# Low-part keys of the second block's attention with 128 rows instead of 64

## The chip, the cores and the metric

The kernel runs on one core of a Trainium2 chip. The metric is the device time of one execution in microseconds (us). Five engines work side by side: TensorE (PE; PEld is its weight load), VectorE (DVE), ScalarE (ACT), GpSimd (POOL) and SyncE (SP), which issues the DMAs.

## What is computed

One forward pass of two transformer blocks over 256 tokens of width 1024. The first block has one layer (a linear recurrence beside sparse attention, then a gated feed-forward). The second has two layers, run over the tokens `x` and a context `ctx` of 256 tokens each. The change lies in the two attentions of the second block's layers: a neighbourhood attention with 4 heads (`A`) and a grouped-query attention with 8 query and 2 key heads (`C`), all of 64 features. The x queries see the keys of x and of the context; the context's queries (first layer only) see the context's alone.

```python
# neighbourhood attention, per row of the grid
s_lat = jnp.einsum('bjqhd,bjykhd->bhjqyk', q_r, k_blk) * scale
s_lat = jnp.where(valid, s_lat + bias, NEG_INF)
s_ctx = jnp.einsum('bjqhd,bchd->bhjqc', q_r, k_ctx) * scale
p = jax.nn.softmax(jnp.concatenate([s_lat, s_ctx], axis=-1), axis=-1)
...
# grouped queries
s = jnp.einsum('bqkgd,bskd->bkgqs', q, k) * (q.shape[-1] ** -0.5)
p = jax.nn.softmax(s, axis=-1)
return jnp.einsum('bkgqs,bskd->bqkgd', p, v)
```

## The kernel before

**Split numbers.** Matmuls take a reduced float32 form (`fp32r`). To keep float32 accuracy, an operand is held as a high part and a low part, the rest that the high part misses, and a product is made of three: high x high, low x high, high x low. In the large projections (`gemm`, L364 to L366) these are three matmuls per tile of 128 rows. A head of the attention has only 64 features, so the queries (`QA`, `QC`) are tiles of 128 rows: rows 0 to 63 hold the high part, rows 64 to 127 the low part. The high-part keys (`KH` for attention A, `CH` for C) lie twice in their 128 rows. So one matmul of 128 rows (L1357) gives high x high plus low x high. The third product, high query x low key, takes the low-part keys (`KL`, `CL`), which fill rows 0 to 63 of a tile allocated with 128 rows (`kv_alloc`): L1362 multiplies rows 0 to 63 of the query tile with rows 0 to 63 of the keys. In the trace the key tiles are named KHa and KLa (attention A) and KHc and KLc (attention C), with a last letter x or c for the tokens that they belong to.

**Units.** `attend` runs over units (head, half of the queries). `soft` makes the scores of 128 queries: for each set of keys 256 columns, by L1357, for attention A's x keys two matmuls for the bias (L1360, L1361), and L1362. So a unit has 2 score matmuls in the context's attention, 4 in x's attention C, 6 in x's attention A. Then VectorE takes the maximum (L1364), ScalarE the exponential and its sum (L1367), VectorE divides (L1368, L1369). `turn`, two units later, transposes the result on TensorE (L1378) and copies it (ScalarE, L1381); after four units, 16 matmuls of the values follow (L1388).

**Where they run.** The context's attention of layer 0 runs from about 804 to 896 us, beside block 1's feed-forward; x's of layer 0 from about 1100 to 1196, beside the context's output projection; x's of layer 1 from about 2075 to 2157. There the only other work is the first half of x's own output projection and what is left of the keys and pooled columns.

**What sets the order.** The program is handed to a scheduler that fixes one order for each engine from a model of its own. The engines then run their lists strictly in order, and wait for each other through semaphores. Scores lie in one set of PSUM buffers (`m`, 4 of them), transposes in another (`f`, 3).

Of the kernel before, what the change touches and what calls it, by code (L numbers as in the profile page):

```python
# [17 lines left out]
PSUM = bass.MemoryType.PSUM  # L18
# [11 lines left out]
# the work of the three mixers: projections, and then what goes beside the units of either attention (a group for each).  # L30
# q, k, v, c, u: projections; V, C, U: what one of their tiles still needs; b: bias; t: a step from outside; s: statistics
# [106 lines left out]
def stat(w, c0, c1):  # L138
    """[K, M] columns c0:c1 as stationary pieces of 128 columns: [M/128, 128, K/128, 128]."""
    w = np.asarray(w)[:, c0:c1]  # L140
    k, m = w.shape
    return np.ascontiguousarray(w.reshape(k // 128, 128, m // 128, 128).transpose(2, 1, 0, 3))


def movp(w):
    """[1024, 512] as moving pieces of 2 row tiles: [4, 128, 2, 512]."""
    w = np.asarray(w)
    return np.ascontiguousarray(w.reshape(4, 2, 128, w.shape[1]).transpose(0, 2, 1, 3))


def upw(a, b):
    """gate and up columns, interleaved by tile: [22, 2, 128, 8, 128]."""
    return np.ascontiguousarray(np.stack([stat(a, 0, FF), stat(b, 0, FF)], 1))


def per_piece(g):
    """column tiles in a down piece of g row tiles"""
    return 1 if g > 4 else 2 if g > 2 else 4


def dnw(w, groups):
    """[2816, 1024]: for each group of row tiles and few column tiles, [128, g, n * 128], one after another."""
    w = np.asarray(w).reshape(NF, 128, 8, 128)
    out, f0 = [], 0
    for g in groups:
        nd = per_piece(g)
        out.append(np.ascontiguousarray(w[f0:f0 + g].reshape(g, 128, 8 // nd, nd * 128).transpose(2, 1, 0, 3)).ravel())
        f0 += g
    return np.concatenate(out)


def adaw(w):
    """[1024, 9216]: pieces [72, 128, 1024] in the order of their use: two modulations at a time, in four parts"""
    w = np.asarray(w).reshape(8, 128, 9216)
    out = []
    for i in range(4):
        a = w[:, :, i * 2048:(i + 1) * 2048]
        for k in range(8):
            out.append(a[k, :, 0:1024])
            out.append(a[k, :, 1024:])  # L180
    for k in range(8):
        out.append(w[k, :, 8192:])
    return np.ascontiguousarray(np.stack(out))
# [82 lines left out]
def build(tc, A, O, dbg=(), stop=None):  # L266
# [32 lines left out]
    f32 = lambda a: a.bitcast(F32)  # L299
# [33 lines left out]
    class Stream:  # L333
# [8 lines left out]
        def load(self, src, a, b, i=0):  # L342
            """a piece as it is; other rings than the usual one take the i-th of many at once"""
            if i < self.nr:
                r = tl(self.raw, [128, 1024], tag="r")
            else:
                r = f32(tl((self.h, self.l)[i % 2], [128, 1024], F32R, tag="hl"[i % 2]))
            rv = r[:, 0:a * b].rearrange("p (a b) -> p a b", a=a)
            self.q.dma_start(rv, src)
            return rv  # L350
# [9 lines left out]
    def gemm(pt, w, m0, m1, xs):  # L360
        """pt += columns m0:m1 of a split stationary piece, over the tiles xs of (hi, lo)"""
        n = len(xs)
        for k in range(n):
            te.matmul(pt, w[0][:, k, m0:m1], xs[k][0], start=k == 0, stop=False)  # L364
            te.matmul(pt, w[0][:, k, m0:m1], xs[k][1], start=False, stop=False)  # L365
            te.matmul(pt, w[1][:, k, m0:m1], xs[k][0], start=False, stop=k == n - 1)  # L366
# [13 lines left out]
    def squares(pp, ps, src, n, late=0, nb=3, scale=None):  # L380
        """sums [128, n / 128] of the squares of src(k), k = 0..7, token-major; the last, late of them, are summed
        by the tensor engine alone"""
        nt = n // 128
        ss = ps(nt)

        def total(sq, first, last):
            for t in range(nt):
                te.matmul(ss[:, t:t + 1], sq[:, t * 128:(t + 1) * 128], ones[:, 0:1], start=first and t == 0, stop=last,
                          skip_group_check=True)

        early = KD - late
        for k in range(KD):
            sq = tl(pp, [128, n], tag="sq", bufs=nb) if k or not early else tl(pp, [128, n], tag="sa", bufs=1)
            s.activation(sq, src(k), AF.Square, scale=scale(k) if scale else 1.0)
            if k == 0:
                acc = sq
            elif k < early:
                g.tensor_tensor(acc, acc, sq, op=OP.add)  # L398
            if k >= early:
                total(sq, k == 0, k == KD - 1)  # L400
            elif k == early - 1:
                total(acc, True, not late)
        return ss

    def stats(pp, ps, src, n, rs, late=0, nb=3):
        """rs [128, n / 128] = 1 / rms of src(k), k = 0..7, token-major"""
# [4 lines left out]
    def rms(pp, ps, src, n, out, late=0, rs=None):  # L411
        """out(k, bc): bc [128, n] is 1 / rms of src(k), k = 0..7, along the columns"""
# [7 lines left out]
        bc = ps(n)  # L420
# [4 lines left out]
    def norm_split(pp, ps, src, n, yh, yl, sc, sh=None, late=0, rs=None):  # L425
        """src * rstd * sc(k) + sh(k) in parts yh, yl"""
# [57 lines left out]
    # ================= block 1 =================  # L484
    def block1(ps, early, ready):
# [8 lines left out]
        # rope tables from the positions  # L494
# [48 lines left out]
        for _ in range(E0):  # L543
            next(early, None)
        with ExitStack() as e:
# [10 lines left out]
            def rope_in(dst, nh, cos, sin, rows=128, pp=pp):  # L556
                """dst [rows, nh, 64] in place"""
# [9 lines left out]
            # token-major queries, then keys and values  # L567
# [57 lines left out]
            # feature-major: receptance, keys, values, low-rank inputs  # L625
# [30 lines left out]
            # compressed keys and values  # L656
# [143 lines left out]
        with ExitStack() as e:  # L800
# [16 lines left out]
            # decay: log w = -e^-0.5 sigmoid(w0 + tanh(w_lat) w2); running sums in each chunk  # L817
# [21 lines left out]
            def head_rstd(sq, scale, eps, floor, neg):  # L839
                """sum of sq over the 64 features of a head -> (.)^-0.5, over the features of the head, in PSUM"""  # L840
# [22 lines left out]
            # negated, normalised keys  # L863
# [15 lines left out]
            # the bonus r . k_mod r_k, over v  # L879
# [9 lines left out]
            # A~ = -kk P_{t-1}, R~ = r P: [pair, token tile, which, token]  # L889
# [20 lines left out]
            # token-major A~, B^, K^, V  # L910
# [20 lines left out]
            # Gram blocks, transposed [j, i]  # L931
# [28 lines left out]
            # (I - L)^-1 by substitution: a partition is (parity of the columns, head, chunk)  # L960
# [92 lines left out]
            # group norm over a head, bonus, gate  # L1053
# [31 lines left out]
    def block1_out(ps, st, before_last):  # L1085
        mix = b1mix
        xr = lambda k: res[:, k, 0:T]
# [1 line left out]
        with ExitStack() as e:  # L1089
# [20 lines left out]
            # the scale of the output norm, and of the norm that follows it on its result  # L1110
# [11 lines left out]
    # ================= block 2 =================  # L1122
# [14 lines left out]
    class Ada:  # L1137
        """modulations of a layer, feature-major: M [128, 9, 8, (x, ctx)], and GS = g (1 + scale) of its three norms"""
# [45 lines left out]
    # each table's rope rows, with the norm's gains (and the queries' 1/8) folded in  # L1184
# [22 lines left out]
    def qkn(pp, src, nh, seg, t, tab, hl):  # L1207
        """heads [128, nh, 64]: norm, rope, split into hl [128, nh, 2, 64]"""
# [28 lines left out]
    def kv_alloc(kp, n):  # L1237
# [4 lines left out]
        o.CL = tl(kp, [128, 2, T], F32R, name="KLc" + n)  # L1242
        o.VA = tl(kp, [128, 2, 256], name="VA" + n)
# [45 lines left out]
    def in_v(l, st, pp, ps, yh, yl, segs, kvs, tab):  # L1289
        """values and keys; returns what is left to do for the keys, a token tile at a time"""  # L1290
# [27 lines left out]
    def in_qc(l, st, pp, ps, yh, yl, seg, t0, tab, QC):  # L1318
        """queries; returns what is left to do, a token tile at a time"""
# [24 lines left out]
    def attend(pp, ps, pst, pso, Q, nh, keys, vals, kvof, mh, ml, bias=None, tick=None):  # L1344
        """keys: [(KH, KL)], vals(i, kt, kv) -> [128, 64]; mh, ml [128, nh / 2, 256]"""
# [5 lines left out]
        def soft(h, t):  # L1351
# [3 lines left out]
            for i, (kh, kl) in enumerate(keys):  # L1355
# [6 lines left out]
                te.matmul(o, q[0:64], kl[0:64, kv], start=False, stop=True)  # L1362
# [39 lines left out]
    class Bias:  # L1402
        """the neighbourhoods' bias and mask of (head, token tile) units, in parts, made some units ahead"""
# [22 lines left out]
    def in_u(l, st, pp, ps, yh, yl, c0, mh, ml):  # L1426
        """pooled columns; returns what is left to do, half of the groups at a time"""
# [34 lines left out]
    def mixer(l, seg, st, qp, side, ps, pin, pst, pso, yh, yl, c0, segs, kvs, tab, mixt, orders, out=True, tick=None, extra=None):  # L1462
        """projections of the sequences segs, attention, pooling and output projection of seg; its columns start at c0"""
# [63 lines left out]
    def norm_mod(l, j, seg, pp, ps, yh, yl, late=0, rs=None):  # L1527
        """modulated norm j of a sequence's residual"""
# [12 lines left out]
    def out_proj(l, seg, st, ps, mixt, half):  # L1541
        """one half of the mixed rows, two column tiles a step"""
# [22 lines left out]
    class Both:  # L1565
        i = 0
# [14 lines left out]
    # the context of block 2's first layer does not wait for block 1: its pools lie at the other end of the memory  # L1581
# [53 lines left out]
    # x, first layer  # L1635
# [37 lines left out]
    # both, to the second layer's projections; x goes ahead of the context at each norm  # L1673
# [79 lines left out]
```

## Time and profile before

| | us |
|---|---|
| median of 3 runs | 2380.18 |
| the runs | 2373.62, 2380.18, 2383.07 |
| span of the profiled execution | 2382.3 |
| TensorE busy | 2283.6 (96%) |
| VectorE busy | 1374.2 (58%) |
| ScalarE busy | 946.8 (40%) |
| GpSimd busy | 361.0 (15%) |

For the profiled execution the page gives the span alone, from the first to the last instruction; its time as a run is not listed. A matmul's busy time is from its start to a modelled end, and one starts before the other has ended, so what it occupies is read from start to start. TensorE has two clock levels, 1.2 and 2.4 GHz; the profile tells the granted share (1.00 or 0.50 of full speed, and a mean where a stretch has both).

### The profile page before, as it was taken

To read this page: it belongs to the slowest core of one execution; us is meant where nothing else is said; L and a number is where in the kernel's file an instruction comes from. 1 tells how busy PE (TensorE), PEld (TensorE's weight loads), DVE (VectorE), ACT (ScalarE), POOL (GpSimd) and SP (SyncE) were. 2 spreads that over 40 slices of the span, in tenths; PEclk is the share of its full clock that TensorE was granted. 3 is DMA by queue.
4 is the path that set the end of the run, shared out by engine and by line. 5 is a ranking of instruction groups with operands and counts; after the bars stand their busy time and mean duration, and the time that the engine had idled before them with its cause. 6 is when DMAs were issued, how large, how long until landed. Compare 5 with 4: busy or idle time off the path is not lost.

```text
span 2382.3 us, 38350 instructions
## 1 busy us (share of the span) xinstructions
PE 2283.6 (96%) x15317; PEld 1964.1 (82%) x15317; DVE 1374.2 (58%) x2442; ACT 946.8 (40%) x1602; POOL 361.0 (15%) x278
## 2 busy tenths in 40 slices
PE   7999987999999899998999999999999999999998
PEld 3687766888999689997778777798888889778998
DVE  4555566358656766677565333357534347855665
ACT  4334422236444454454543222245322235554443
POOL 2125444444101200002010000011000003200000
PEclk9999998999999899997999999999999999989999
DMA  8865544356554145553166434465523245303554
GB/s 295 283 213 177 177 129 145 108 176 225 181 179 166 62 141 176 174 175 104 41 221 223 159 131 165 138 236 187 195 92 98 92 134 178 116 21 100 185 186 131
DMA packets 114929, 376.25 MB, mean 158 GB/s; under 512 B 18464, under 2 KB 24480, under 8 KB 114752
## 3 DMA queue, kind: packets, MB, share of 16 engines
q1 hardware_dynamic: 114752, 373.82, 47.3%
q8 instruction: 120, 1.97, 0.3%
q14 instruction: 57, 0.47, 0.1%
HBM read 372.20 MB, written 1.57 MB: 157 GB/s over the span
## 4 chain that ended last, share of the span: by engine, by line
PE 65%; issue 23%; DVE 6%; DMA 4%; POOL 1%; ACT 1%; SPq 0%; POOLq 0%; DVEq 0%; ACTq 0%
PE m L364 10%; PE m L366 10%; PE m L365 10%; PE f L364 5%; PE f L366 5%; PE f L365 5%; PE f L1163 3%; DMA r<-in_ada 2%; PE o L1388 2%; PE m L1362 2%; PE f L1378 1%; PE m L1357 1%; POOL sa L398 1%; DVE l L357 1%; ACT h L356 1%
## 5 line engine op out<-in xcount | busy, mean ns | idle before, releaser
L356 ACT CAST h<-r 128x1024 fp32r<-128x1024 f32 (+1 forms) x547 | 567.1, 1042 | 1065.4 <-PE m L365 434.9
L357 DVE TENSOR_TENSOR l<-r,h 128x1024 fp32r<-128x1024 f32 (+1 forms) x467 | 572.3, 1229 | 352.2 <-ACT h L356 343.0
L364 PE MATMUL m<-yh,h 128*128 128x256 f32 (+1 forms) x1624 | 490.2, 303 | 2.3 <-ACT h L356 1.1
L366 PE MATMUL m<-yh,l 128*128 128x256 f32 (+1 forms) x1624 | 489.8, 302 | 1.0 <-DVE l L357 1.0
L365 PE MATMUL m<-yl,h 128*128 128x256 f32 (+1 forms) x1624 | 489.5, 302 | 0.0
L364 PEld LDWEIGHTS m<-yh,h 128*128 128x128 f32 x1624 | 310.1, 192 | 25.9 <-ACT h L356 8.1
L366 PEld LDWEIGHTS m<-yh,l 128*128 128x128 f32 x1624 | 310.2, 191 | 19.8 <-issue 7.1
L365 PEld LDWEIGHTS m<-yl,h 128*128 128x128 f32 x1624 | 310.4, 191 | 15.6 <-issue 3.7
L357 POOL TENSOR_TENSOR l<-r,h 128x1024 fp32r<-128x1024 f32 x80 | 194.2, 2432 | 337.7 <-ACT h L356 318.6
L398 POOL TENSOR_TENSOR sa<-sa,sq 128x256 f32<-128x256 f32 x81 | 86.1, 1064 | 1038.5 <-issue 743.6
L365 PE MATMUL m<-hl,h 128*128 128x256 f32 (+1 forms) x738 | 220.1, 302 | 0.0
L366 PE MATMUL m<-hh,l 128*128 128x256 f32 (+1 forms) x738 | 219.9, 303 | 0.0
L364 PE MATMUL m<-hh,h 128*128 128x256 f32 (+1 forms) x738 | 215.6, 304 | 0.1
L364 PE MATMUL f<-yh,h 128*128 128x256 f32 (+1 forms) x624 | 199.6, 320 | 1.8 <-ACT yh L434 1.1
L365 PE MATMUL f<-yl,h 128*128 128x256 f32 (+1 forms) x624 | 198.0, 317 | 1.2 <-DVE yl L435 1.2
L366 PE MATMUL f<-yh,l 128*128 128x256 f32 (+1 forms) x624 | 197.8, 317 | 0.0
L364 PE MATMUL f<-hh,h 128*128 128x256 f32 (+1 forms) x446 | 138.7, 316 | 14.4 <-DVE ft L461 6.7
L366 PEld LDWEIGHTS m<-hh,l 128*128 128x128 f32 x738 | 139.1, 189 | 8.5 <-issue 1.6
L365 PEld LDWEIGHTS m<-hl,h 128*128 128x128 f32 x738 | 139.7, 189 | 6.7 <-issue 0.4
L364 PEld LDWEIGHTS m<-hh,h 128*128 128x128 f32 x738 | 136.3, 189 | 10.1 <-issue 2.1
L1538 DVE SCALAR_TENSOR_TENSOR res<-m,mod,res 128x256 f32<-128x256 f32 x176 | 79.3, 479 | 111.3 <-PE m L366 111.1
L366 PE MATMUL f<-hh,l 128*128 128x256 f32 (+1 forms) x446 | 135.6, 311 | 1.5 <-POOL l L357 1.5
(509 smaller groups left out, 4120.2 us busy)
## 6 DMA issues: line engine op xcount, KB each, us to landing
r<-in_up SPq DMA_DIRECT2D x252, 512.0 KB, 3.6
r<-in_ada SPq DMA_DIRECT2D x144, 512.0 KB, 4.4
r<-in_dn SPq DMA_DIRECT2D x98, 512.0 KB, 3.6
r<-in_w1u SPq DMA_DIRECT2D x44, 512.0 KB, 3.5
r<-in_dn SPq DMA_DIRECT2D x32, 448.0 KB, 3.3
r<-in_w2m SPq DMA_DIRECT2D x24, 512.0 KB, 4.0
r<-in_w2o SPq DMA_DIRECT2D x24, 512.0 KB, 3.5
r<-in_w1d SPq DMA_DIRECT2D x22, 512.0 KB, 3.5
```

The costliest lines, as they stand in the source:

```text
L356: s.copy(h, r)
L357: self.e.tensor_tensor(l, r, f32(h), op=OP.subtract)
L364: te.matmul(pt, w[0][:, k, m0:m1], xs[k][0], start=k == 0, stop=False)
L365: te.matmul(pt, w[0][:, k, m0:m1], xs[k][1], start=False, stop=False)
L366: te.matmul(pt, w[1][:, k, m0:m1], xs[k][0], start=False, stop=k == n - 1)
L398: g.tensor_tensor(acc, acc, sq, op=OP.add)
L1163: te.matmul(pt[j * 32:j * 32 + 32], adac[:, k], w[j], start=k == 0, stop=k == KD - 1)
L1357: te.matmul(o, q, kh[:, kv], start=True, stop=False)
L1362: te.matmul(o, q[0:64], kl[0:64, kv], start=False, stop=True)
L1378: te.transpose(pT[:, b * 128:b * 128 + 128], P[:, b * 128:b * 128 + 128], ident)
L1388: te.matmul(po[j * 64:j * 64 + 64], vals(b // 2, b % 2, kvof(2 * pr + j)), PT[j][:, b], start=b == 0, stop=b == nt - 1)
L1538: v.scalar_tensor_tensor(r, pt[:, i * T:i * T + T], ad[l].M[:, m, d, q:q + 1], r, op0=OP.mult, op1=OP.add)
```

## The change

The low-part keys get all 128 rows: at allocation, GpSimd sets rows 64 to 127 of the tiles `KL` and `CL` to zero (8 memsets in all, four pairs: context and x of layer 0, x and context of layer 1), and the third score matmul takes the whole query tile and all 128 rows of the keys. The low part of the query then meets the zeros.

```diff
@@ kv_alloc
         o.CL = tl(kp, [128, 2, T], F32R, name="KLc" + n)
+
+        g.memset(f32(o.KL)[64:128], 0.0)
+        g.memset(f32(o.CL)[64:128], 0.0)
         o.VA = tl(kp, [128, 2, 256], name="VA" + n)
...
@@ attend
-                te.matmul(o, q[0:64], kl[0:64, kv], start=False, stop=True)
+                te.matmul(o, q, kl[:, kv], start=False, stop=True)
```

The rest of the diff empties lines of comments and docstrings. No other instruction is added or dropped; lines behind `kv_alloc` move down by 3, so L1362 becomes L1365. The engines' orders stay as they were but for the memsets and a few neighbours that change places in three spots.

GpSimd, layer 0, the norm of x ahead of its projections, before (`sa`: sums of squares; L409 makes `rs`, 1/rms; `pu`: pooled columns; `hss`: norms of heads):

```order
L398 TENSOR_TENSOR sa_11537<-sa_11537,sq_11539 128x256
L398 TENSOR_TENSOR sa_11537<-sa_11537,sq_11542 128x256
L409 TENSOR_TENSOR rs_11535<-rs_11535,mhalf_69 128x2
L1435 MEMSET pu_12012 128x8
L1436 MEMSET pu_12012 128x8
```

and now:

```order
L398 TENSOR_TENSOR sa_11541<-sa_11541,sq_11543 128x256
L398 TENSOR_TENSOR sa_11541<-sa_11541,sq_11546 128x256
L1244 MEMSET KLax_11388 64x1024
L1245 MEMSET KLcx_11390 64x512
L409 TENSOR_TENSOR rs_11539<-rs_11539,mhalf_69 128x2
L1438 MEMSET pu_12016 128x8
```

The pair of memsets has come between the last sum and the power behind it.

VectorE, layer 1, the second tile of grouped queries (`hx`, `hq`: normed and turned queries) beside the low-part keys, before; on GpSimd the layer's second pair of memsets stands ahead of the power for this query tile (`hss`):

```order
L1232 TENSOR_TENSOR hl_20622<-hq_20631,hl_20622 128x8x64
L1217 TENSOR_TENSOR hx_20658<-qraw_20445,hss_20654 128x512
L1340 CAST QC_20295<-m_20639 128x4x128
L357 TENSOR_TENSOR l_20717<-r_20714,h_20716 128x1024
L1229 TENSOR_TENSOR hq_20660<-hx_20658,cgq_19691 128x512
L1287 TENSOR_TENSOR KLax_19718<-m_20525,KHax_19717 64x256
L357 TENSOR_TENSOR l_20747<-r_20744,h_20746 128x1024
```

and now:

```order
L1232 TENSOR_TENSOR hl_20630<-hq_20639,hl_20630 128x8x64
L1343 CAST QC_20303<-m_20647 128x4x128
L357 TENSOR_TENSOR l_20725<-r_20722,h_20724 128x1024
L1217 TENSOR_TENSOR hx_20666<-qraw_20453,hss_20662 128x512
L1290 TENSOR_TENSOR KLax_19722<-m_20533,KHax_19721 64x256
L357 TENSOR_TENSOR l_20755<-r_20752,h_20754 128x1024
```

The first step of the second query tile (L1217, reading `hss`) has gone behind a copy of finished queries and one weight split.

## Rows read from the trace of the kernel before

**Rows 1.** The page: busy time of each engine, and the chain's shares by engine.

```profile
PE 2283.6 (96%) x15317; PEld 1964.1 (82%) x15317; DVE 1374.2 (58%) x2442; ACT 946.8 (40%) x1602; POOL 361.0 (15%) x278
...
PE 65%; issue 23%; DVE 6%; DMA 4%; POOL 1%; ACT 1%; SPq 0%; POOLq 0%; DVEq 0%; ACTq 0%
```

**Rows 2.** Timeline of TensorE, context's attention (start, length, engine, line, tiles, shape):

```profile
836.95 0.28 PE L366 MATMUL m<-yh,l 128*128 128x256 f32 x1
837.07 0.28 PE L1357 MATMUL f<-KHcc,QC 128*128 128x256 f32 x1
837.28 0.38 PE L1362 MATMUL f<-KLcc,QC 64*128 64x256 f32 x1
837.59 0.38 PE L364 MATMUL m<-yh,h 128*128 128x256 f32 x1
837.81 0.28 PE L365 MATMUL m<-yl,h 128*128 128x256 f32 x1
```

**Rows 3.** The same of layer 0's grouped queries of x, one unit's start and the next's.

```profile
1145.79 0.39 PE L1357 MATMUL m<-KHcx,QC 128*128 128x256 f32 x1
...
1147.04 0.39 PE L1357 MATMUL m<-KHcx,QC 128*128 128x256 f32 x1
```

**Rows 4.** The same at low clock: a neighbourhood unit, then filler matmuls.

```profile
1102.89 0.58 PE L1357 MATMUL m<-KHax,QA 128*128 128x256 f32 x1
...
1104.85 0.58 PE L1362 MATMUL m<-KLac,QA 64*128 64x256 f32 x1
1105.36 0.58 PE L1357 MATMUL m<-KHax,QA 128*128 128x256 f32 x1
...
1120.30 0.41 PE L365 MATMUL f<-mixl,h 128*128 128x256 f32 x1
1120.51 0.41 PE L366 MATMUL f<-mixh,l 128*128 128x256 f32 x1
...
1120.93 0.28 PE L365 MATMUL f<-mixl,h 128*128 128x256 f32 x1
```

**Rows 5.** L1362 by stretch: stretch, length, PE, PEld, granted clock, DMA, GB/s.

```profile
803.80:814.00 10.20, 2.32 (x4) 1.14 (x4) 0.51 0.00 1
814.00:896.00 82.00, 7.62 (x20) 3.65 (x20) 1.00 0.36 116
1100.00:1117.20 17.20, 6.93 (x12) 3.42 (x12) 0.50 0.13 44
1117.20:1196.00 78.80, 13.75 (x37) 6.58 (x36) 0.95 0.15 48
2075.00:2077.00 2.00, 0.76 (x2) 0.37 (x2) 0.91 0.54 217
2077.00:2108.00 31.00, 10.42 (x18) 5.13 (x18) 0.51 0.05 13
2108.00:2157.00 49.00, 10.69 (x28) 5.12 (x28) 1.00 0.10 33
```

**Rows 6.** All work by stretch: length, busy PE, PEld, DVE, ACT, POOL, granted clock, DMA.

```profile
814.00:896.00 82.00, 81.60 (x585) 70.22 (x583) 56.62 (x130) 43.94 (x101) 0.00 (x0) 1.00 0.36 116
1100.00:1117.20 17.20, 17.20 (x50) 11.82 (x48) 10.67 (x29) 5.63 (x14) 4.31 (x6) 0.50 0.13 44
1117.20:1196.00 78.80, 77.08 (x469) 58.84 (x469) 45.81 (x99) 39.02 (x84) 0.71 (x1) 0.95 0.15 48
2077.00:2108.00 31.00, 31.00 (x93) 20.50 (x93) 16.40 (x45) 13.01 (x37) 3.69 (x5) 0.51 0.05 13
2108.00:2157.00 49.00, 49.00 (x305) 36.03 (x306) 28.77 (x63) 27.02 (x59) 0.00 (x0) 1.00 0.10 33
```

**Rows 7.** GpSimd: groups of memsets (busy, mean ns, idle before), then two timeline rows.

```profile
L967 POOL MEMSET TT<- 128x1024 f32 x2 | 1.8, 952 | 0.0
L812 POOL MEMSET SB<- 128x512 f32 x2 | 1.1, 588 | 3.6 <-PE o L787 3.6
...
1044.32 0.71 POOL L409 TENSOR_TENSOR rs<-rs,mhalf 128x2 f32<-128x2 f32 x1 [7.07 <-DVE rs L408]
...
2045.81 1.74 POOL L1215 TENSOR_TENSOR hss<-hss,mhalf 128x8 f32<-128x8 f32 x1 [4.53 <-DVE hss L1214]
```

## The prediction

> **What bounds the kernel now.** I began with the page. TensorE is busy for 96% of the span and holds 65% of the chain of work that ended last [rows 1]. So time taken from TensorE is time taken from the end, unless another engine is next in line at that place. The change touches one line of matmuls, L1362, so I read how far apart matmuls start around it; durations are no help, since matmuls overlap and their ends are modelled. In the context's attention [rows 2], the rows run L366, L1357, L1362, L364, L365. From L366 to L1357, both of 128 rows, 0.12 us pass. To the 64-row L1362 it is 0.21 us, from it to the next 0.31, and from that one to the one after it 0.22. The tile names show that L364 belongs to other work (block 1's feed-forward), so the delay is not a dependence between the two score matmuls. A 64-row matmul among 128-row ones thus delays three starts. A unit of the x attention has two of them: L1357 to the next unit's L1357 takes 1.25 us for four matmuls [rows 3].
>
> Then I asked at what clock each stands. The table by stretch counts L1362: 86 of the 120 lie in stretches with a granted clock near 1.0 (2.4 GHz) and 34 near 0.5 (1.2 GHz) [rows 5]. In the low stretches a unit of six matmuls takes 2.47 us, from 1102.89 to 1105.36, while 128-row matmuls at the same clock start 0.21 us apart (1120.30, 1120.51) [rows 4]. TensorE's lane is full in nearly all of these stretches, and VectorE and ScalarE are not [rows 6].
>
> **The score matmuls.** Their number, columns (256) and order on TensorE stay; the added 64 rows are zero. The price is the pitch.
> At full clock: 0.21 + 0.31 + 0.22 = 0.74 us for what three 128-row starts do in 3 x 0.12 = 0.36; 0.38 us each. The x unit says the same: 1.25 - 4 x 0.12 = 0.77 for two. 86 x 0.38 = 32.7 us.
> At half clock: 2.47 - 6 x 0.21 = 1.2 us for two, 0.6 each. 34 x 0.6 = 20.4 us.
> TensorE's work falls by 53 us. The bounds of a single price are 0 (the delay has another cause) and these values. I take these values, because the same 256 columns at 128 rows stand directly beside the slow ones.
>
> Here a rule speaks against the change. The row first: L366 and L1357 both have 128 rows and start 0.12 us apart [rows 2]. The Trainium skill, "TensorE: Matmul & The Clock Gate", section "What overlaps and what doesn't", says that a weight load overlaps running matmuls only where the row group differs. By that rule the 128-row form could not be faster than the 64-row one and the gain would be 0; the row contradicts it.
>
> How much of the 53 lies on the path, stretch by stretch [rows 5, 6]:
> - 814 to 896 (context; 20 matmuls): 7.6 us off TensorE leaves 74.4, VectorE has 56.6 of work. All 7.6 count. The freed lane takes block 1's feed-forward earlier.
> - 803.8 to 814 (4, half clock): here TensorE already waits. Of 2.4 I take 1.0.
> - 1100 to 1117.2 (12, half clock): 17.2 - 7.2 = 10.0, below VectorE's 10.67, so VectorE becomes the bound and at most 6.5 can come. I take 4.5, since its work also waits for its turn.
> - 1117.2 to 1196 (36; the table's 37 has one that overlaps the edge): 13.7 off leaves 65.1 against 45.8 on VectorE. All 13.7.
> - 2075 to 2108 (2 and 18): 0.8 + 10.8. In 2077 to 2108, 31.0 - 10.8 = 20.2 is left against VectorE's 16.4. That is tight, so I take nine tenths, 10.5 together.
> - 2108 to 2157 (28): 10.6 off leaves 38.4 against 28.8. All 10.6.
> Sum: 7.6 + 1.0 + 4.5 + 13.7 + 10.5 + 10.6 = 47.9 us.
>
> **The clock.** From 2077 to 2108 TensorE is busy throughout and is granted 0.51 [rows 6]. It did not get the full clock back while it ran score units with 64-row matmuls; at 1120.9 it did get it back (durations 0.41 to 0.28) while it ran a row of 128-row ones [rows 4]. With 128-row scores the units look like the latter, so full clock may return earlier. Price: 2077 to 2108 cannot shrink below VectorE's 16.4 us, which is 20.2 - 16.4 = 3.8 plus the 1.1 I did not count above; and the matmuls between 1117.2 and 1120.9, at 0.21 apart instead of 0.12, are worth about 1.6. So 0 to 6.5 us; a loss is a rival below. I take 4, nearer to the upper end, as the row at 1120.9 is the nearest thing to the new state.
>
> **The eight memsets.** The nearest rows are GpSimd's 128-partition ones: 0.95 us for 1024 columns, 0.59 for 512 [rows 7]. Four pairs make 6.2 us. They wait for what lay in that memory before, and GpSimd's later work queues behind them. In layer 0's x norm, the pair stands ahead of the power that makes 1/rms (1044.32): GpSimd was idle for 7.07 us there, more than a pair's 1.5, and the normalisation of x waits behind it. In layer 1 it stands ahead of the second query tile's power (2045.81), with 4.53 us idle; who waits for that is the query chain on VectorE, whose first step falls one place back there. I take 0, hidden by that idleness; if a cover is gone, a pair costs 1.5, so 0 to 6.2 in all. The high-part copies and key subtractions do not wait for the zeros, since they write other partitions.
>
> **Sum.** 47.9 + 4 = 52 us. The profiled execution's span is 2382.3; 2382.3 - 52 = 2330. The span is 2.1 us above the median of the three runs (2380.18), so I put the forecast at 2380.2 - 52 = 2328.
>
> **Rival 1: the rows are not the cause.** Then the pitch stays and the time is 2380. For it: in these rows every matmul of 64 rows is of this line, so shape and line can't be told apart by them. The Trainium skill says as much: the page named above, section "Why this matters for your kernels", has a matmul of few rows take the same time as one of 128. By that rule the time stays 2380. Against it: L1357 has the same query tile, output tile, column count and type, and starts at 0.12 beside 128-row neighbours [rows 2]. 4%.
>
> **Rival 2: softmax takes the place.** TensorE runs ahead and waits for the maximum, the exponential and the scaling of the unit two back. Then the context's 7.6 still come (feed-forward fills), but of the other 40 only half: 7.6 + 20 = 27.6, 2353. For it: in 1100 to 1117 VectorE is already next. Against: elsewhere VectorE and ScalarE would still have a quarter of the time free [rows 6]. 9%.
>
> **Rival 3: slower, by the clock.** The shorter units leave TensorE waiting for softmax, and it is granted 1.2 GHz in stretches that now have 2.4: 1117 to 1196 and 2108 to 2157, where 65.1 + 38.4 = 103.5 us of work are left. At 0.21 instead of 0.12 a start this becomes 78 us longer: 2328 + 78 = 2406. It decides from 52 / 0.75 = 69 us of work at the low level; from there on the kernel is slower. For it: the layer 1 loop drops from 0.91 to 0.51 at 2077 [rows 5]. Against: 1117 to 1196 holds 0.95 although TensorE idles there for 1.7 us [rows 6], and there is filler work (the output projections) between the units. 4%.
>
> **How the numbers follow.** Forecast (2314 to 2347) 83%, rival 2 9%, rival 1 4%, rival 3 4%. The lower end, 2314: all 53, the clock's 6.5 and some 6 for the spread of single runs (2373.6 to 2383.1). The upper end, 2347: seven tenths of 47.9 and no clock gain, 33 us. That leaves a little under 2 in 10 outside. What a measurement of this kernel tells from no change is about 0.5%, 12 us: forecast and rival 2 are both faster by more, 92%; within 4%; slower 4%.
>
> **What would show it.** In the changed trace: the low-part matmul with 128 rows, 0.12 us after the high-part one and 0.12 before the next; an x unit of four in about 0.5 us; the L1362 group's successor no more among the costly ones of the chain; stretches shorter by about 8 (context), 18 to 20 (layer 0) and 21 to 25 (layer 1); the layer 1 stretch at 0.5 shorter than 31 us; GpSimd with eight more memsets that nobody waits for. Wrong would be: a pitch that stays at 0.3 (rival 1), idle time on TensorE before the transposes in the units (rival 2), a granted clock near 0.5 after 1120 or 2108 (rival 3), or a gain outside these three stretches, which no term here explains.

## The result, and the profile after

The changed kernel takes 2324.61 us (median of 4 runs, 2315.94 to 2327.26); the kernel before, measured beside it, 2379.30 us. The ratio is 0.976, with a 95% interval of 0.974 to 0.978. The forecast was 2328 us in a range of 2314 to 2347.

The page of the profile after, its lines for busy time and for the chain by engine:

```profile
PE 2226.8 (96%) x15317; PEld 1943.0 (84%) x15317; DVE 1367.7 (59%) x2442; ACT 944.8 (41%) x1602; POOL 367.5 (16%) x286
...
PE 76%; issue 11%; DVE 7%; DMA 3%; POOL 2%; ACT 1%; SPq 0%; POOLq 0%; DVEq 0%; ACTq 0%
```

Against [rows 1], TensorE has the same number of instructions and is busy for 56.8 us less, about what the span lost (2382.3 to 2324.7). GpSimd has the eight memsets more (286 against 278). The fall of "issue" from 23% of the chain to 11% is not this gain: it is some 290 us, of which one piece of 331 us (from 1640.7 us, far from the attentions) is in the chain before and not in the chain after, and the kernel below that keeps 64 rows and the old time has 9%. The delayed starts stood under the names of the matmuls around them: in the chain of layer 1's x attention, L1362 and L1357 hold 21.2% and 17.1% before, and L1365 and L1360, the same lines, 6.8% and 6.9% after.

The starts themselves, first in the context's attention, then in a grouped unit of x (timeline of TensorE: start, length, engine, line, tiles, shape). They answer [rows 2] and [rows 3]:

```profile
834.53 0.28 PE L366 MATMUL m<-yh,l 128*128 128x256 f32 x1
834.64 0.28 PE L1360 MATMUL f<-KHcc,QC 128*128 128x256 f32 x1
834.76 0.28 PE L1365 MATMUL f<-KLcc,QC 128*128 128x256 f32 x1
834.88 0.28 PE L364 MATMUL m<-yh,h 128*128 128x256 f32 x1
835.00 0.28 PE L365 MATMUL m<-yl,h 128*128 128x256 f32 x1
...
1126.29 0.28 PE L1360 MATMUL m<-KHcx,QC 128*128 128x256 f32 x1
1126.41 0.28 PE L1365 MATMUL m<-KLcx,QC 128*128 128x256 f32 x1
1126.53 0.28 PE L1360 MATMUL m<-KHcc,QC 128*128 128x256 f32 x1
1126.65 0.28 PE L1365 MATMUL m<-KLcc,QC 128*128 128x256 f32 x1
1126.77 0.60 PE L1381 MATMUL f<-cst,P 128*128 128x128 f32 x4
```

Every start is 0.12 us from the last; the unit of four takes 0.48 us where it took 1.25. At low clock a neighbourhood unit of six takes 1.28 us (1095.60 to 1096.88) where [rows 4] has 2.47, and the clock then returns: the lengths fall from 0.41 to 0.28 within the third unit:

```profile
1095.60 0.41 PE L1360 MATMUL m<-KHax,QA 128*128 128x256 f32 x1
...
1096.88 0.41 PE L1360 MATMUL m<-KHax,QA 128*128 128x256 f32 x1
...
1097.41 0.28 PE L1365 MATMUL m<-KLax,QA 128*128 128x256 f32 x1
```

Where the time went: the three attention stages, each from its first score matmul to its last grouped value matmul (layer 1's rows begin 0.2 us earlier, with a pair of transposes; table by stretch: stretch, length, busy PE, PEld, DVE, ACT, POOL with their instructions, granted clock, share of DMA, GB/s). Before:

```profile
803.88:908.00 104.12, 103.33 (x707) 87.94 (x705) 73.09 (x172) 55.03 (x128) 5.53 (x5) 0.95 0.34 108
1100.45:1200.30 99.85, 98.12 (x546) 73.65 (x546) 56.32 (x128) 45.83 (x100) 4.75 (x6) 0.88 0.13 43
2074.68:2162.20 87.52, 87.52 (x447) 62.55 (x449) 46.83 (x113) 42.17 (x100) 4.90 (x8) 0.82 0.11 35
```

After:

```profile
804.41:900.30 95.89, 94.53 (x707) 86.05 (x705) 72.94 (x172) 54.88 (x128) 5.54 (x5) 0.95 0.34 118
1094.18:1169.70 75.52, 72.32 (x546) 61.76 (x546) 54.67 (x128) 44.85 (x100) 5.13 (x6) 0.98 0.16 57
2041.78:2104.60 62.82, 60.92 (x449) 50.72 (x451) 45.25 (x113) 41.45 (x100) 4.92 (x8) 0.97 0.14 48
```

They hold the same work (707, 546 and some 448 matmuls) and are 8.2, 24.3 and 24.7 us shorter, 57.2 of the 57.6 us. Two things show in these rows: the granted clock of the x stages rose from 0.88 to 0.98 and from 0.82 to 0.97, and TensorE's gaps in them grew from 1.7 us and none to 3.2 and 1.9 us.

### The profile page after: what moved, and what is told of

Read it like the earlier page. It is cut to its first block, busy times and chain, and to the rows that moved or that the text cites. A ratio compares the mean times of both kernels' runs of the same rounds, so it can differ in the third digit from the quotient of the medians.

```text
span 2324.7 us, 38368 instructions
## 1 busy us (share of the span) xinstructions
PE 2226.8 (96%) x15317; PEld 1943.0 (84%) x15317; DVE 1367.7 (59%) x2442; ACT 944.8 (41%) x1602; POOL 367.5 (16%) x286
## 4 chain that ended last, share of the span: by engine, by line
PE 76%; issue 11%; DVE 7%; DMA 3%; POOL 2%; ACT 1%; SPq 0%; POOLq 0%; DVEq 0%; ACTq 0%
PE m L364 13%; PE m L366 13%; PE m L365 13%; PE f L364 7%; PE f L366 7%; PE f L365 7%; PE f L1163 4%; PE o L1391 2%; POOL sa L398 1%; DMA r<-in_ada 1%; PE f L1381 1%; DVE l L357 1%; DVE tm L972 1%; ACT h L356 1%; DMA r<-in_up 1%
## 5 line engine op out<-in xcount | busy, mean ns | idle before, releaser
L366 PEld LDWEIGHTS m<-yh,l 128*128 128x128 f32 x1624 | 310.4, 191 | 18.2 <-issue 7.1
L365 PEld LDWEIGHTS m<-yl,h 128*128 128x128 f32 x1624 | 310.6, 191 | 15.4 <-issue 3.7
L398 POOL TENSOR_TENSOR sa<-sa,sq 128x256 f32<-128x256 f32 x81 | 86.2, 1064 | 907.3 <-ACT sq L394 490.0
L1541 DVE SCALAR_TENSOR_TENSOR res<-m,mod,res 128x256 f32<-128x256 f32 x176 | 79.1, 478 | 105.5 <-PE m L366 105.0
L365 PE MATMUL f<-hl,h 128*128 128x256 f32 (+1 forms) x446 | 136.8, 309 | 0.3 <-DVE hl L370 0.3
```

Of the source, the lines that this page charges most:

```text
L1541: v.scalar_tensor_tensor(r, pt[:, i * T:i * T + T], ad[l].M[:, m, d, q:q + 1], r, op0=OP.mult, op1=OP.add)
```

## Experiments

Each time is the median of the runs; the kernel before, measured beside each set, had 2380.68, 2378.57 and 2380.34 us. Stage lengths are read as above, from the first score matmul to the last grouped value matmul.

| kernel | time, us | ratio to before, 95% | context | layer 0, x | layer 1, x |
|---|---|---|---|---|---|
| before | 2380 | | 104.1 | 99.9 | 87.5 |
| changed | 2324.61 | 0.974 to 0.978 | 95.9 | 75.5 | 62.8 |
| zeros alone | 2379.92 | 0.998 to 1.002 | 103.7 | 101.3 | 85.7 |
| 128 rows where there is no bias | 2347.46 | 0.982 to 0.987 | 95.9 | 86.2 | 75.5 |
| 128 rows where there is a bias | 2357.81 | 0.987 to 0.993 | 105.0 | 91.3 | 73.7 |
| 96 rows | 2323.87 | 0.972 to 0.977 | | | |
| low part twice, 64 rows | 2396.33 | 1.006 to 1.010 | | | |
| low part twice, 128 rows | 2339.98 | 0.980 to 0.985 | | | |
| low beside low, 64 rows | 2356.42 | 0.987 to 0.993 | 105.1 | 86.9 | 76.9 |
| changed, modulations two by two | 2341.27 | 0.982 to 0.988 | | | |
| changed, its buffers alone | 2329.23 | 0.976 to 0.982 | | | |

### The zeros alone

```
-                te.matmul(o, q, kl[:, kv], start=False, stop=True)
+                te.matmul(o, q[0:64], kl[0:64, kv], start=False, stop=True)
```

> The changed kernel with the low-part matmul put back to 64 rows; the eight memsets stay. Theory (the pitch of the 64-row matmul is the whole cause): within 0.3% of the kernel before, about 2380 us, the low-part matmul again at 0.21 us after the high-part one and 0.31 before the next, the clock low again for about 17 us in layer 0 and 31 in layer 1. Rival (part of the gain comes from the memsets, which shift GpSimd's work and the small swaps in the order): some of the 55 us stays, under 2370.

Measured: 2379.92 us, no difference. The memsets and the few swaps in the engines' orders cost nothing and bring nothing that shows, and the 64-row pitch is back. So is the low clock, with other lengths than expected: 20 us from the first score matmul in layer 0 (17 expected) and 27 us in layer 1 (31 expected). TensorE's timeline in the context's attention of this kernel:

```profile
848.25 0.28 PE L1360 MATMUL f<-KHcc,QC 128*128 128x256 f32 x1
848.46 0.38 PE L1365 MATMUL f<-KLcc,QC 64*128 64x256 f32 x1
848.77 0.38 PE L366 MATMUL m<-hh,l 128*128 128x256 f32 x1
```

0.21 and 0.31 us, as in [rows 2]. The whole gain hangs on the form of this one matmul.

### 128 rows in one of the two attentions

```
+                if bias is None:
                     te.matmul(o, q, kl[:, kv], start=False, stop=True)
+                else:
+                    te.matmul(o, q[0:64], kl[0:64, kv], start=False, stop=True)
```

and the other way round (`if bias is not None`) in a second kernel.

> 128 rows only in the grouped attention (80 of the 120 matmuls), the neighbourhood attention stays at 64 rows. Theory: 48 + 28 matmuls at full clock by 0.38 us and 4 at half clock by 0.6 make 31 us; the neighbourhood loops keep the low clock as before, until the grouped units begin; 2348 us (2343 to 2353). Rival (the low clock has nothing to do with the 64-row matmuls, it follows what lies ahead of the loops): the high clock returns at another time than in the kernel before although the neighbourhood loop is untouched.

> 128 rows only in the neighbourhood attention (40 of the 120 matmuls). Theory (pitch and clock): the rest of the changed kernel's gain, 55 - 31 = 24 us, 2356 us, with half-clock stretches of about 3 us in layer 0 and layer 1 as in the changed kernel. Rival (pitch alone, the clock as before): 0.6 us for some 32 and 0.38 for 8, of which VectorE hides a part, 18 us, 2362 us, with half-clock stretches of 17 and 31 us less the pitch.

The split fell a little otherwise than these texts say: the context's neighbourhood attention has no bias, so its 8 matmuls went with the grouped ones, and the counts are 88 and 32. Measured: 2347.46 and 2357.81 us, gains of 33.2 and 22.9 us. They add up to 56.1, the whole change. The 32 matmuls with a bias are worth only 17.9 us by their pitch (12 at 0.6 and 4 at 0.38 in layer 0, 14 and 2 in layer 1), of which VectorE would hide a part. The time alone does not settle what the other 5 us are, as the interval of that gain is 17.6 to 31.2 us; the granted clock shows the difference. The table by stretch at the start of layer 1's x attention, in the kernel before, in the kernel with 128 rows where there is no bias, where there is a bias, and in the changed kernel (granted clock third from the end):

```profile
2076.00:2107.50 31.50, 31.50 (x95) 21.07 (x95) 17.40 (x48) 13.75 (x38) 3.99 (x7) 0.51 0.05 14
```

```profile
2048.00:2078.00 30.00, 29.05 (x86) 20.65 (x87) 15.88 (x48) 13.50 (x38) 5.13 (x8) 0.50 0.09 31
```

```profile
2072.00:2076.00 4.00, 4.00 (x22) 3.95 (x21) 3.97 (x13) 2.84 (x10) 1.68 (x3) 0.58 0.25 76
```

```profile
2042.00:2046.00 4.00, 4.00 (x23) 4.00 (x22) 3.53 (x11) 2.72 (x8) 1.67 (x4) 0.59 0.39 145
```

The low clock lasts some 30 us where the neighbourhood units have 64-row matmuls, and under 4 us where they have not (the 28 us behind the last two rows have 1.00), whatever the grouped units do. TensorE's lane is full or nearly full in all of the low stretches, so within them no idle time shows that would hold the clock down.

The rival of the first text, that the low clock follows what lies ahead of the loop, is out for its length. For its beginning it is not. Right ahead of layer 1's loop TensorE has nothing to do for 3.33 us, in the kernel before (the row below) as in the changed one (up to 2041.78), and the granted clock falls 2 and 1 us behind that gap:

```profile
2074.68 0.44 PE L1309 MATMUL m<-cst,hl 128*128 128x128 f32 x2 [3.33 <-DVE hl L1232]
```

In the kernel "changed, its buffers alone", also with 128 rows, the same gap of 3.33 us stands there and the clock stays at 1.00 in the 10 us behind it, so the gap does not always bring the fall. In the kernel before, the clock came back both times in a row of matmuls none of which has 64 rows: the filler matmuls of [rows 4] (from 1117.53) and the value matmuls of 128x64 (from 2104.74).

### 96 rows

```
-                te.matmul(o, q, kl[:, kv], start=False, stop=True)
+                te.matmul(o, q[0:96], kl[0:96, kv], start=False, stop=True)
```

> The low-part matmul over 96 rows (rows 64 to 95 of the keys zero, the query tile's rows 0 to 95). Theory (it is the use of half of the rows that TensorE treats apart, and 96 rows are treated as 128): 2325 us, 0.12 us pitch. Rival (any number of rows other than its neighbours' 128 delays the starts): 2380 us, pitches of 0.21 and 0.31 as with 64.

Measured: 2323.87 us, the time of the changed kernel. Its timeline in the context's attention:

```profile
828.12 0.28 PE L1360 MATMUL f<-KHcc,QC 128*128 128x256 f32 x1
828.24 0.28 PE L1365 MATMUL f<-KLcc,QC 96*128 96x256 f32 x1
828.36 0.28 PE L364 MATMUL m<-yh,h 128*128 128x256 f32 x1
```

96 rows among 128 start like 128 rows. So it isn't that the number of rows differs from the neighbours'; 64 rows are another form to TensorE and 96 are not. Rows between 64 and 96 were not tried.

### The low part twice

```
+                te.matmul(o, q[0:64], kl[0:64, kv], start=False, stop=False)
                 te.matmul(o, q[0:64], kl[0:64, kv], start=False, stop=True)
```

and the same with 128 rows in the changed kernel.

> The kernel before with each 64-row low-part matmul issued twice in a row (the low part is added twice, so the output is off by that). Theory (the delay belongs to the change of form, 128 to 64 rows and back): the second one starts 0.12 us after the first at full clock and 0.21 at half, 86 x 0.12 + 34 x 0.21 = 17 us more, about 2396 us. Rival (each 64-row matmul carries the delay by itself): the second one starts 0.3 or more after the first, 45 to 55 us more, about 2430 us.

> The changed kernel with each 128-row low-part matmul issued twice (the low part is added twice, so the output is off by that). Theory (a 128-row one costs its 256 columns and no more): 0.12 us each, 120 x 0.12 = 14 us less what VectorE hides in the neighbourhood loops, 2336 to 2340 us. Rival (reading the zero rows has a price of its own that the change hides elsewhere): over 2345 us.

Measured: 2396.33 us, 17.8 more than before, which is 0.148 us for each of the 120 added matmuls (0.11 to 0.20 by the interval); 86 starts of 0.12 and 34 of 0.21 make 0.146. So the second 64-row matmul costs its columns and has no delay of its own. The context's timeline (L1363 is the second one):

```profile
891.47 0.28 PE L1357 MATMUL f<-KHcc,QC 128*128 128x256 f32 x1
891.68 0.38 PE L1362 MATMUL f<-KLcc,QC 64*128 64x256 f32 x1
891.90 0.27 PE L1363 MATMUL f<-KLcc,QC 64*128 64x256 f32 x1
892.11 0.39 PE L365 MATMUL m<-yl,h 128*128 128x256 f32 x1
892.33 0.28 PE L366 MATMUL m<-yh,l 128*128 128x256 f32 x1
```

From L1357 four starts take 0.21 + 0.22 + 0.21 + 0.22 = 0.86 us, where [rows 2] has 0.74 for three: 0.12 more for one matmul more. The second one starts 0.22 after the first and not the 0.12 that was expected, but the one behind it comes 0.10 sooner. With 128 rows the second copy costs 2339.98 - 2324.61 = 15.4 us or 0.128 each, as nearly all of them run at full clock there.

### Low beside low

```
             for i, (kh, kl) in enumerate(keys):
                 o = pS[:, i * T:i * T + T]
+                if i:
+                    te.matmul(o, q[0:64], kl[0:64, kv], start=True, stop=False)
+                    te.matmul(o, q, kh[:, kv], start=False, stop=True)
+                    continue
```

> The kernel before, 64 rows and no zeros, but for the second key set of an x unit the low part goes ahead of the high part: high, low, low, high in the place of high, low, high, low. So 48 pairs of 64-row matmuls stand side by side; nothing is added or left out. Theory (the delay belongs to the change between 64 and 128 rows, of which each of the 48 units now has one pair less): 34 x 0.38 + 14 x 0.6 = 21 us less, about 2359 us. Rival (each 64-row matmul carries it): no change, 2380 us.

Measured: 2356.42 us, 23.9 less than before, with the same instructions at the same 64 rows. The delay belongs to the change from one form to the other. A grouped unit of this kernel, and the next work behind it:

```profile
1137.81 0.36 PE L1361 MATMUL m<-KHcx,QC 128*128 128x256 f32 x1
1138.11 0.38 PE L1366 MATMUL m<-KLcx,QC 64*128 64x256 f32 x1
1138.33 0.28 PE L1358 MATMUL m<-KLcc,QC 64*128 64x256 f32 x1
1138.54 0.39 PE L1359 MATMUL m<-KHcc,QC 128*128 128x256 f32 x1
1138.76 0.60 PE L1382 MATMUL f<-cst,P 128*128 128x128 f32 x4
```

The unit takes 0.95 us: 0.47 more than 128 rows throughout (0.48) and 0.30 less than high, low, high, low (1.25). The low stretch of layer 1 lies between the others too:

```profile
2057.00:2081.00 24.00, 23.60 (x79) 18.18 (x80) 15.01 (x44) 11.77 (x34) 5.14 (x8) 0.51 0.11 38
```

24 us, against 27 to 34 with twice as many changes of form (27 with the zeros alone, 31 before, 34 with the low part twice at 64 rows) and 4 with none. In layer 0 it is 14 us from the first score matmul, against 20 before and 3 in the changed kernel.

### Modulations two by two: a test that didn't come about

```
-                for j in range(4):
-                    te.matmul(pt[j * 32:j * 32 + 32], adac[:, k], w[j], start=k == 0, stop=k == KD - 1)
+                held.append(w)
+                if k % 2:
+                    for j in range(8):
+                        te.matmul(pt[j % 4 * 32:j % 4 * 32 + 32], adac[:, k - 1 + j // 4], held[j // 4][j % 4], start=k + j // 4 == 1, stop=k + j // 4 == KD)
+                    held = []
...
-    st_c = Stream("sc", 3, 2, side=R, stack=rs, eng=g, parts=rs2)
+    st_c = Stream("sc", 4, 2, side=R, stack=rs, eng=g, parts=rs2)
```

This was to carry the finding to L1163, whose groups of four matmuls have 32 stationary columns.

> The changed kernel, and in the modulations (L1163, groups of four matmuls with 32 stationary columns) two groups at a time, eight in a row, so that there are half as many places where 128x128 matmuls and these meet; for that the weights have a ring of 4 tiles in the place of 3, and the first context norm has one buffer where it had three. Theory (the delay of such a change is there for fewer columns too): a group of four costs 1.17 us among 256-column matmuls, 512 columns alone some 0.85, so 0.3 us for each of up to 80 places, 18 to 24 us less than the changed kernel, 2301 to 2307 us. Rival (these groups wait for their weights, or the early loads delay others): 2320 to 2335 us.

> The control for the run with two modulation groups at a time: the changed kernel with the ring of 4 tiles and the single buffers of the first context norm alone, the groups of four as before. Theory: within 0.3% of the changed kernel, 2318 to 2332 us. Rival (the ring of 4 lets loads start earlier, and that is what the other run gains): 2301 to 2310 us.

Measured: 2341.27 us, slower than the changed kernel by 17; the buffers alone gave 2329.23, within their 0.3%. It is no verdict on columns, because the pairs did not hold together: the program's order on TensorE is worked out from when the weights are expected, and in many pairs it put the last two of the eight matmuls behind other work. A group of the changed kernel, and the two parts of one pair (the count at the row's end has two records for each matmul):

```profile
1328.45 0.39 PE L366 MATMUL f<-yh,l 128*128 128x512 f32 x1
1328.77 1.06 PE L1163 MATMUL f<-r,sc 128*32 128x512 f32 x8
1329.77 0.50 PE L364 MATMUL m<-yh,h 128*128 128x512 f32 x1
```

```profile
1328.37 1.91 PE L1166 MATMUL f<-r,sc 128*32 128x512 f32 x12
1330.21 0.50 PE L364 MATMUL m<-yh,h 128*128 128x512 f32 x1
...
1336.37 1.05 PE L1166 MATMUL f<-r,sc 128*32 128x512 f32 x4
1337.35 0.50 PE L366 MATMUL m<-yh,l 128*128 128x512 f32 x1
```

A group takes 1.00 us from its start to the next matmul, the pair 1.84 + 0.98. The group starts 0.32 us after the matmul ahead of it, where matmuls of 512 columns start 0.22 to 0.23 us apart there, so a delay stands at this change of form too; what pairing would save stays open. Six matmuls and then two cost more than four and four, and the places where the forms meet fell only from 104 to 95, not to half. Whether that is all of the 17 us was not followed up.

## Why the prediction held, and where its sizes were off

**The price of a start** was right. 0.38 us at full clock came from three delayed starts beside 128-row ones, and after the change all three are 0.12. At low clock the unit of six lost 2.47 - 1.28 = 1.19 us, which is 0.6 each. The cause was a change of form, and three runs say so from three sides: a second 64-row matmul beside the first costs 0.148 us, putting two side by side gives back 24 us, and 96 rows cost nothing extra.

**The context**: 7.6 + 1.0 = 8.6 us expected, 8.2 measured.

**The clock, and the bound by VectorE in the loops,** are the terms that were mis-sized. The terms by pitch were put at 18.2 us in layer 0 (4.5 + 13.7) and 21.1 in layer 1 (10.5 + 10.6). The stages lost 24.3 and 24.7, so 6.1 + 3.6 = 9.7 us lie above them, where the sum has 4 for the clock and its upper end 6.5. But not all of that is the clock's. The neighbourhood loops from their first score matmul to a place behind them, before and after, in layer 0 (to the first filler matmul) and in layer 1 (to the third grouped unit):

```profile
1100.45:1117.53 17.08, 17.08 (x49) 11.70 (x48) 10.79 (x30) 5.63 (x14) 4.04 (x5) 0.50 0.10 34
1094.18:1103.25 9.07, 7.77 (x48) 6.96 (x47) 9.07 (x26) 5.22 (x13) 3.44 (x4) 0.83 0.18 58
```

```profile
2074.88:2108.30 33.42, 33.42 (x106) 22.25 (x106) 18.05 (x50) 14.86 (x41) 4.70 (x8) 0.54 0.08 25
2041.97:2060.88 18.91, 17.01 (x106) 13.62 (x106) 16.62 (x50) 14.67 (x41) 4.72 (x8) 0.91 0.13 45
```

They lost 8.0 and 14.5 us, where the sum has 4.5 and 10.5. The whole pitch, with nothing taken off for VectorE, is 7.2 and 11.6, so 3.8 of the 9.7 us are pitch that the sum had taken off. In layer 0 this is a step that failed: "at most 6.5 can come", because VectorE had 10.67 us of work there. VectorE is indeed busy for all of the 9.07 us, but some of its work went behind the loop's end, where TensorE has its filler matmuls. The other 5.9 us go beyond the pitch: 0.8 and 2.9 in the loops, 1.5 in the row of filler matmuls (4.34 to 2.84 us; 1.6 expected) and 0.7 behind, with the dip below. They are put down to the clock; no run held the clock and took the pitch away.

The direction was argued rightly from [rows 4], and the fall of layer 1's low stretch from 31 to 4 us is the sign it named. In layer 0 the price counted only the matmuls between 1117.2 and 1120.9, while the clock now rises 3 us into the loop and nearly all of the loop runs at it. And it left out a second low stretch inside the grouped loop, that stood in the 0.95 of [rows 5] without being asked about. Before, and then the changed kernel's whole grouped loop (by stretch):

```profile
1160.00:1168.00 8.00, 8.00 (x49) 6.42 (x48) 3.50 (x7) 2.47 (x6) 0.00 (x0) 0.79 0.22 68
```

```profile
1111.00:1173.00 62.00, 60.89 (x470) 50.79 (x469) 38.35 (x86) 38.02 (x85) 0.71 (x1) 1.00 0.16 57
```

At 0.79 over 8 us the loop loses 8 x 0.21 = 1.7 us. Of the kernels looked at there, the dip is in those whose grouped units of x change form four times (before, zeros alone, 128 rows where there is a bias, low part twice with 64 rows), and not in those where they change twice or never (low beside low; 128 rows where there is no bias; the changed kernel).

**VectorE as the next bound** in layer 0's neighbourhood loop was right as a sign: in the 9.07 us above VectorE has no gap, and TensorE is busy for 7.77. This is rival 2 at one place, and it is worth the 1.3 us between these numbers there, not half of the x stages. TensorE's longest waits in the x attentions are 1.4 us in two for the exponential (L1370) and 1.0 us for a part of the bias in layer 1. Behind the loops TensorE is busy throughout in layer 1 (43.72 us from 2060.88) and for 60.89 of 62.00 us in layer 0.

**The memsets** were right at 0. Each pair takes 1.5 us and none stands in the chain that ended last. The pair in the norm of x, where GpSimd has nothing to do between the sum and the power [rows 7]:

```profile
1026.63 2.88 POOL L398 TENSOR_TENSOR sa<-sa,sq 128x256 f32<-128x256 f32 x2 [120.08 <-ACT sq L394]
1029.56 0.95 POOL L1244 MEMSET KLax<- 64x1024 f32 x1
1030.45 0.52 POOL L1245 MEMSET KLcx<- 64x512 f32 x1
```

A memset of 64 partitions takes as long as one of 128 with the same columns (0.95 us for 1024), so the price from [rows 7] could be taken over as it was.

**Rivals 1 and 3.** Rows are the cause: with the zeros but 64 rows the time is 2380. By the rule cited there from the Trainium skill, "TensorE: Matmul & The Clock Gate", section "Why this matters for your kernels", few rows take the time of 128. For a lone 64-row matmul among 128-row ones the runs disagree by 0.38 us; for the second of two in a row, 0.148 us against 0.146, they agree. The Trainium skill, "TensorEngine Tiling (Array Packing)", section "Key Properties", does foresee a cost: changing the tiling mode drains TensorE. The runs agree that a change costs, 0.38 us for a lone one and back at full clock; that a drain is what takes the time, they do not show. The loss by the clock did not come: it went the other way.

**The total**: 52 us expected, 54.7 between the medians measured side by side and 57.6 between the two profiled spans, which are what the terms are made against. Of these 5.6 us too few, 3.5 are the loop of layer 0 (8.0 for 4.5) and 2.2 the rest above the pitch terms (6.2, less the 4 of the clock); the context is 0.4 too high, and outside the stages 0.4 went.

## What to carry to other kernels

Read the starts, not the durations: a matmul of another array form costs its neighbours' starts. The lengths show only half of it (in [rows 2] two of 0.38 us instead of 0.28, for a delay of 0.38), and the chain's "issue" does not show it at all. Where a 64-row matmul stands alone among 128-row ones, fill its rows with zeros if the memory is there; if not, put such matmuls side by side, which here gave 24 of the 54.7 us with no instruction added. When a loop runs at the low clock although TensorE is busy throughout, look for idle time right ahead of it, behind which the clock fell here, and for such changes of form in it, with which the low clock lasted longer.

## What the runs showed of the hardware that was not expected

- 96 rows among 128-row matmuls start at 0.12 us like 128; 64 rows do not.
- The length of the low-clock stretch followed the changes of form in the loop: 27 to 34 us in layer 1 with four in a unit of x, 24 with two, and with none 4 or no fall at all, behind the same gap of 3.33 us and at a TensorE lane that reads as busy in nearly all of it. What links the two was not separated: the units with changes are also slower, and no run slowed TensorE in another way.
- The second of two 64-row matmuls starts 0.22 us after the first, not 0.12; the delay of a lone one, 0.38, is only spread otherwise over the starts behind it.
